# Last scan group's norms in fewer pieces, a ninth early block in the up projection, and a fourth buffer for weight differences

## The chip, the cores and the metric

The kernel runs on one core of a Trainium2 chip. The metric is device time in microseconds of one execution of the whole program, taken as the median of several runs. The profile of one execution shows five engines: PE (TensorE, matmuls) with its weight loads PEld, DVE (VectorE), ACT (ScalarE), POOL (GpSimd) and SP (SyncE), which issues DMAs.

## The reference

One layer of a two-branch encoder over 1024 rows of width 1024, float32. Cut to what the change touches:

```python
# branch B, the scan: forward and backward, 8 groups of 256 columns, 8 chunks of 128 rows
y = y_fwd + y_bwd + d_skip[:, None] * xs
y = y.reshape(b, l, D_INNER) * jax.nn.silu(z)
yg = y.reshape(b, l, SSD_GROUPS, D_INNER // SSD_GROUPS)
yg = yg * lax.rsqrt(jnp.mean(yg * yg, axis=-1, keepdims=True) + EPS)
...
merged = sigmoid(gate_a) * (attn @ w_attn_branch) + sigmoid(gate_b) * (ssd @ w_ssd_branch)
x = x + merged @ w_out
x = x + cross_attention(...)
h = rmsnorm(x, norm_ffn)
x = x + jnp.square(jax.nn.relu(h @ w_up)) @ w_down      # w_up 1024 x 4096
```

## The kernel before

The phases follow each other: the scan branch together with the gates' projection, attention, merge, cross attention, the up projection, the down projection. Every float32 matmul is three fast ones on a high and a low part (`mm3`, lines 83, 87 and 88); ACT writes the rounded high part and DVE or POOL the remainder. PE's order is as the code writes it; on the other engines a scheduler sets the order, and `issue_after(x)` keeps what is issued under it behind instruction x on the engine of x alone.

**The scan.** `step(q, c)` does chunk c of group q: a mask product (`cb`), products into the same tile, and `yo`, which needs a PSUM bank of a pool "p" of four that the gates' projection (`gps`, line 83 and on) shares. DVE and POOL finish the chunk (`yz`), ACT squares and sums it (`zs`, line 631). When four chunks are done, `rstd_of` gives their norm (DVE `rv`, line 120; POOL power `rr`, line 122) and ACT scales each `yz`. `yt(q)` transposes the four into two banks (line 650), and ACT copies these out (`yts`, line 652). The steps of the last group run between the products of the last gate jobs: `job(gate_job(10), {3: [...]})` puts its calls behind the job's third group of three matmuls. In the last group chunks 7 to 4 are normed together, and each of chunks 3 to 0 alone (`norm_one`, line 643), one step late.

**The up projection.** It is one level of the Strassen-Winograd scheme: 16 blocks of w_up's columns, each a "quad" of seven products of 12 matmuls (line 1412), in the order P1, P2, P6, P5, P7, P3, P4. P1 and P2 need only the input as it is; the others need sums of its quarters (`s1` to `s4`), which `sums` makes as the input rows become ready. So `ahead` does P1 and P2 of some blocks early, between the calls of `sums`: x = P1 is stored (`u`), P1 + P2 is added (line 1441) and squared (lines 1417 and 1418, ACT). Such a block's quad comes last, has five products, and fetches x back. The weights come in 512 KB loads on SP's queue (`raw`, two buffers and two shared ones); `right` makes a quad's differences t5 to t8 on DVE (lines 1385, 1386, 1388, 1391), and `put` splits each on ACT and POOL into `wop` (six buffers, lines 1357 and 1358). `start(order, 5)` issues the first five operands of the quads, `more` one more behind each product. The stores of results, the fetches and the weight loads are all issued by SP, one behind the other.

In the quads, line 1474 copies P1, line 1477 adds P2, line 1489 adds P7 (`c22`), line 1464 adds x in the quads of early blocks, and line 1493 adds P3. During the last three quads the first rows of the down projection are loaded (`sraw`) and split.

Of the kernel before, what the change touches and what calls it, by code (L numbers as in the profile page):

```python
# [16 lines left out]
P = 128  # L17
# [432 lines left out]
def ssd_phase(kx, ins, dr):  # L450
# [4 lines left out]
    with tc.tile_pool(name="p1", bufs=1) as sp, tc.manual_schedule(engines={mybir.EngineType.PE}):  # L455
# [138 lines left out]
        def step(q, c):  # L594

            b, j = c // 4, c % 4
            cl = slice(c * P, (c + 1) * P)
            cb, ef = q.cb, q.efs[c]
            if c:
                mask(q, c - 1)  # L600
            if c > 1:
                prep(q, c - 2)
            if j == 3:
                q.yz, q.ss = [None] * 4, sp.tile([P, 4], F32, tag="ss", bufs=2, name="ss")
            for h in range(4):
                PE.matmul(cb[:, 256 + 64 * h:256 + 64 * h + 64], ef[:, h], q.xtok[:, c, 64 * h:64 * h + 64],  # L606
                          start=True, stop=True)
            lo, hi = (256 if c == 0 else 0), (256 if c == NT - 1 else 512)
            yo = kx.pp.tile([P, 512], F32, tag="p", name="yo")
            PE.matmul(yo[:, lo:hi], q.CT[:, cl], q.prev[:, c].rearrange("p d q -> p (d q)")[:, lo:hi],  # L610
                      start=True, stop=True)
            d0, d1 = lo // 256, hi // 256
            t = sp.tile([P, 2, 256], F32, tag="t", bufs=1, name="t")
            V.tensor_tensor(t[:, d0:d1].rearrange("p d (h q) -> p d h q", h=4),
                            yo[:, lo:hi].rearrange("p (d h q) -> p d h q", h=4, q=64),
                            kx.ecs[:, b, j, d0:d1, q.hs].unsqueeze(3).broadcast_to([P, d1 - d0, 4, 64]), ALU.mult)
            single = q.g == NG - 1 and b == 0
            if single and j < 3:
                norm_one(q, j + 1)
            p1 = sp.tile([P, 256], F32, tag="p1", bufs=2, name="p1")  # L620
            G.tensor_tensor(heads(p1), heads(q.xtok[:, c]), dsk[:, q.hs].unsqueeze(2).broadcast_to([P, 4, 64]), ALU.mult)
            if d1 - d0 == 2:
                G.tensor_tensor(p1, p1, t[:, 1], ALU.add)
            if c > 1:
                with tc.issue_after(q.shut.ins):
                    back(q, c - 1)
            y = q.yz[j] = sp.tile([P, 256], F32, tag="yz", bufs=8, name="yz")
            V.tensor_tensor(y, cb[:, 256:], t[:, d0], ALU.add)
            V.tensor_tensor(y, y, p1, ALU.add)
            V.tensor_tensor(y, y, q.zs[:, c], ALU.mult)  # L630
            A.activation(q.zs[:, c], y, AF.Square, accum_out=q.ss[:, j:j + 1])
            if single and j == 0:
                norm_one(q, 0)
                q.done = b, q.yz
            elif not single and j == 0:
                r = rstd_of(kx, sp, q.ss, 4, 256, 4 * EPS)
                for i in range(4):
                    A.activation(q.yz[i], q.yz[i], AF.Copy, scale=r[:, i:i + 1])
                q.done = b, q.yz

        def norm_one(q, j):
            r = rstd_of(kx, sp, q.ss[:, j:j + 1], 1, 256, 4 * EPS)
            A.activation(q.yz[j], q.yz[j], AF.Copy, scale=r[:, 0:1])

        def yt(q):
            b, yz = q.done
# [29 lines left out]
            job(z_job(q), at)  # L676
        q = gs[7]
        job(gate_job(8), {5: [(step, q, 7)], 10: [(step, q, 6)], 15: [(step, q, 5)]})
        job(gate_job(9), {4: [(step, q, 4)], 9: [(step, q, 3)], 14: [(step, q, 2)]})
        job(gate_job(10), {3: [(yt, q), (step, q, 1)], 8: [(step, q, 0)]})  # L680
        w = jobs[0][0][0]()
        for n, ((_, run), at) in enumerate(jobs):
            nxt = jobs[n + 1][0][0]() if n + 1 < len(jobs) else None
# [503 lines left out]
def up_phase(kx, ins, dr, ok, grow, x1_low):  # L1187

    nc, tc = kx.nc, kx.tc
    with tc.tile_pool(name="p4", bufs=1, reuse_waits="tile") as mp:  # L1190
# [17 lines left out]
        with tc.tile_pool(name="tp", bufs=1, side="right", reuse_waits="tile") as tp:  # L1208
# [12 lines left out]
            up.sums(2, xns[0])  # L1221
            behind = up.turned
            up.ahead((5,))
            last = up.sums(3, xns[1])
            up.ahead((6, 7), behind)
            order = [b for b in range(16) if b not in up.early] + sorted(up.early)
            with tc.issue_after(last.ins):
                up.start(order, 5)
            stage = []
            for n, b in enumerate(order):  # L1230
                up.scalar = n > 11
                up.skip = 2 * (n == 14)
                if n == 13:
                    us, wd = down_tiles(kx)
                    wd = wd_views(wd[0])
                    raws = []

                    def load(src):
                        raws.append(mp.tile([P, D], F32, tag="ld", bufs=2, name="sraw"))
                        nc.sync.dma_start(raws[-1], src)  # L1240

                    def u_part(j):
                        split_u(kx, None, us, j, raws.pop(0))

                    def w_part(j):
                        split_wd(kx, None, wd[2 * j:2 * j + 2], j, raws.pop(0), nc.vector)

                    loads = [lambda j=j: load(dr.u[j]) for j in range(4)]
                    loads += [lambda j=j: load(ins["wdn"][j]) for j in range(2)]
                    splits = [lambda j=j: u_part(j) for j in range(4)] + [lambda j=j: w_part(j) for j in range(2)]  # L1250
                    stage += [loads[0], loads[1]]
                    for k in range(6):
                        stage.append(splits[k])
                        if k < 4:
                            stage[-1] = lambda k=k: (splits[k](), loads[k + 2]())
                up.quad(b, stage, order[n + 1] if n < 15 else None)
# [42 lines left out]
class Up:  # L1299
# [5 lines left out]
    def __init__(self, kx, ins, dr, mp, tp, s3, grow):  # L1305
        self.kx, self.ins, self.dr, self.mp, self.tp, self.s3, self.grow = kx, ins, dr, mp, tp, s3, grow
        s3["s2"] = kx.mp.tile([P, 4, 2, 512], F32R, tag="kt", bufs=4, name="kt")
        for key in ("s1", "s3", "s4", "a22"):
            s3[key] = mp.tile([P, 4, 2, 512], F32R, tag=key, bufs=1, name=key)
        self.early, self.scalar, self.skip = set(), True, 0  # L1310

    def t2(self, name):
        return self.tp.tile([P, 512], F32, tag="c", bufs=7, name=name)
# [55 lines left out]
    def right(self, order):  # L1369
# [7 lines left out]
        for n, b in enumerate(order):  # L1377
# [3 lines left out]
            if b not in self.early:  # L1381
                yield self.put(b11)
                yield self.put(b21)
            t5, t6, t7 = (self.tp.tile([P, 512], F32, tag="w", bufs=3, name="w") for _ in range(3))
            V.tensor_tensor(t5, b12, b11, ALU.subtract)
            V.tensor_tensor(t6, b22, t5, ALU.subtract)
            yield self.put(t6)
            V.tensor_tensor(t7, b22, b12, ALU.subtract)
            yield self.put(t5)
            yield self.put(t7)  # L1390
            V.tensor_tensor(t6, b21, t6, ALU.subtract)
            yield self.put(b22)
            yield self.put(t6)
            if n == 14:
                nxt = load(15)

# [3 lines left out]
            self.more()  # L1400

    def more(self):
        w = next(self.gen, None)
        if w is not None:
            self.ready.append(w)

# [21 lines left out]
    def ahead(self, bs, behind=None):  # L1428
# [3 lines left out]
        for b in bs:  # L1432
# [5 lines left out]
            kx.nc.scalar.activation(x, pb, AF.Copy)  # L1438
            kx.nc.sync.dma_start(self.dr.u[2 * b + 1][:, :512], x)
            self.product(pd, w[2], 2, True)  # L1440
            kx.nc.vector.tensor_tensor(c11, x, pd, ALU.add)
            self.square(c11, b, 0, 0)
            self.early.add(b)

    def quad(self, b, stage, nxt):
        kx = self.kx
# [438 lines left out]
```

## Time and profile before

| | |
|---|---|
| median of 3 runs | 2322.02 us (2321.02 to 2322.73) |
| the profiled execution: time, span | 2320.58 us, 2318.8 us |
| mean granted clock of PE | 0.996 |
| busy: PE, DVE, ACT, POOL | 2292.3, 1588.0, 1171.9, 932.0 us |
| PE's longest waits | 7.6 us (up projection), 5.2 us (last scan group) |

A line of the timeline reads: start, duration, engine, line of the kernel, operation, output <- inputs, shape, how many were drawn together, and in brackets the idle time of that engine just before and what ended it. A line of the waits gives the waiting tile, the work that ended the waits, the total, how many there were, and the longest. PEclk is the clock that PE was granted, as a share of its full speed.

### The profile page before, as it was taken

The page shows a single profiled execution, that of the slowest core. Times are in us where ns is not written, and L with a number is a line of the kernel's source. Part 1 is how long each engine was busy: PE and PEld are TensorE (multiplying, and loading weights), DVE is VectorE, ACT ScalarE, POOL GpSimd, SP SyncE. Part 2 cuts the span into 40 slices and gives each one's busy share as a digit, 9 for nine tenths or more (in the row PEclk, how much of TensorE's full clock was granted, in tenths as well). Part 3 has the DMA queues.
Part 4 walks back from the last instruction along what each step waited for, and adds up shares of the span by engine and source line. Part 5 has one row for each costly group of instructions (what it writes and reads, how often), then busy time and mean ns, then how long its engine had stood idle before and what let it go on. Part 6 is the DMA issues. An engine that isn't in the chain of part 4 may idle for free.

```text
span 2318.8 us, 32456 instructions
## 1 busy us (share of the span) xinstructions
PE 2292.3 (99%) x11882; PEld 1944.8 (84%) x11882; DVE 1588.0 (68%) x2501; ACT 1171.9 (51%) x2486; POOL 932.0 (40%) x887
## 2 busy tenths in 40 slices
PE   9999999999999999999999999999989999999998
PEld 8888898988889897888888888888968887888887
DVE  5877666677766673467659888865664456589984
ACT  5455655655465555488865442445553334233341
POOL 2355746565564754354540021125664444100010
PEclk9999999999999999999999999999999999999999
DMA  6222324232232323111144257011453345712201
GB/s 234 82 83 92 110 73 118 74 107 85 91 110 73 112 79 100 40 44 37 51 159 173 91 202 250 30 44 63 144 164 109 109 141 184 288 73 98 112 28 73
DMA packets 150322, 251.04 MB, mean 108 GB/s; under 512 B 11409, under 2 KB 86289, under 8 KB 150162
## 3 DMA queue, kind: packets, MB, share of 16 engines
q1 hardware_dynamic: 79408, 210.41, 26.8%
q10 hardware_dynamic: 70754, 38.55, 5.8%
q8 instruction: 94, 1.54, 0.3%
q14 instruction: 66, 0.54, 0.1%
HBM read 201.47 MB, written 47.45 MB: 107 GB/s over the span
## 4 chain that ended last, share of the span: by engine, by line
PE 87%; DVE 4%; ACT 3%; issue 2%; POOL 2%; DMA 2%; ACTq 0%; POOLq 0%; SPq 0%; DVEq 0%
PE mps L1625 10%; PE dps L1625 10%; PE pb L1412 6%; PE cps L83 4%; PE cps L88 4%; PE cps L87 4%; PE pc L1412 3%; PE zp L83 2%; PE zp L88 2%; PE zp L87 2%; PE cb L606 2%; PE yo L610 2%; PE gps L83 2%; PE gps L88 2%; PE gps L87 2%
## 5 line engine op out<-in xcount | busy, mean ns | idle before, releaser
L67 POOL TENSOR_TENSOR wlo<-raw,whi 128x1024 fp32r<-128x1024 f32 x96 | 235.7, 2456 | 385.6 <-ACT whi L64 310.8
L1576 ACT ACTIVATE kt<-row 128x512 fp32r<-128x512 f32 x264 | 143.8, 619 | 183.5 <-PE dps L1625 82.9
L1625 PE MATMUL mps<-kt 128*128 128x512 f32 x1008 | 229.7, 389 | 0.0
L1625 PE MATMUL dps<-kt 128*128 128x512 f32 x1008 | 228.6, 389 | 0.0
L1625 PEld LDWEIGHTS dps<-kt 128*128 128x128 f32 x1008 | 189.2, 188 | 39.3
L1625 PEld LDWEIGHTS mps<-kt 128*128 128x128 f32 x1008 | 189.0, 188 | 39.1
L83 PE MATMUL cps<-kt,whi 128*128 128x512 f32 x512 | 215.2, 420 | 0.0
L88 PE MATMUL cps<-kt,wlo 128*128 128x512 f32 x512 | 200.0, 391 | 0.0
L87 PE MATMUL cps<-kt,whi 128*128 128x512 f32 x512 | 199.2, 389 | 0.0
L64 ACT ACTIVATE whi<-raw 128x1024 fp32r<-128x1024 f32 x104 | 109.6, 1054 | 147.2 <-DMA raw<-in_wa_dram 26.8
L1577 DVE TENSOR_TENSOR kt<-row,kt 128x512 fp32r<-128x512 f32 x264 | 171.4, 697 | 3.8 <-ACT kt L1576 3.7
L548 POOL TENSOR_TENSOR xl<-xs,xh 128x512 fp32r<-128x512 f32 (+1 forms) x64 | 85.9, 1343 | 105.3 <-ACT xh L547 76.9
L122 POOL TENSOR_TENSOR rr<-rv,mhalf 128x1 f32<-128x1 f32 (+1 forms) x52 | 35.6, 686 | 227.5 <-DVE rv L120 220.4
L1358 POOL TENSOR_TENSOR wop<-w,wop 128x512 fp32r<-128x512 f32 x64 | 83.9, 1314 | 91.3 <-ACT wop L1357 83.9
L87 PEld LDWEIGHTS cps<-kt,whi 128*128 128x128 f32 x512 | 96.3, 188 | 25.3 <-issue 6.7
L83 PEld LDWEIGHTS cps<-kt,whi 128*128 128x128 f32 x512 | 96.3, 188 | 25.0 <-issue 6.0
L88 PEld LDWEIGHTS cps<-kt,wlo 128*128 128x128 f32 x512 | 96.1, 188 | 20.7
L583 ACT ACTIVATE ef<-rows,ebias 128x128 f32<-128x128 f32 x256 | 91.1, 393 | 34.7 <-PE cb L606 28.7
L809 DVE CUSTOM_DVE_ANT_0 t<-sps,bias,snk 128x384 f32<-128x384 f32 (+1 forms) x128 | 71.4, 581 | 52.4 <-PE sps L808 51.7
L817 POOL TENSOR_SCALAR t<-t,den 128x384 f32<-128x384 f32 (+1 forms) x128 | 69.2, 560 | 90.2 <-DVE den L815 81.2
L1412 PE MATMUL pb<-kt,wop 128*128 128x512 f32 x384 | 95.8, 399 | 8.1 <-ACT c L1474 7.6
L83 PE MATMUL gps<-kt,whi 128*128 128x512 f32 x240 | 103.7, 432 | 0.0
(393 smaller groups left out, 6491.0 us busy)
## 6 DMA issues: line engine op xcount, KB each, us to landing
rows<-d_cs ACTq DMA_DIRECT2D x128, 256.0 KB, 3.9
raw<-in_wssd_dram SPq DMA_DIRECT2D x48, 512.0 KB, 3.8
raw<-in_wup_dram SPq DMA_DIRECT2D x40, 512.0 KB, 4.1
d_u<-c SPq DMA_DIRECT2D x64, 256.0 KB, 2.3
row<-in_wdn_dram SPq DMA_DIRECT2D x28, 512.0 KB, 6.5
row<-d_u SPq DMA_DIRECT2D x28, 512.0 KB, 6.8
x<-in_x_dram SPq DMA_DIRECT2D x16, 512.0 KB, 6.5
raw<-in_wg_dram SPq DMA_DIRECT2D x16, 512.0 KB, 3.7
```

Source lines behind the costliest of these rows:

```text
L64: steps = [nc.scalar.activation(hi, raw, AF.Copy)]
L67: steps.append((eng or nc.gpsimd).tensor_tensor(lo, raw, hi.bitcast(F32), ALU.subtract))
L83: i = mm(out, l[0], r[0], start=first, stop=False)
L87: mm(out, l[0], r[1], start=False, stop=False)
L88: mm(out, l[1], r[0], start=False, stop=last)
L548: G.tensor_tensor(xl[:, lo:hi], xf[:, lo:hi], xh[:, lo:hi].bitcast(F32), ALU.subtract)
L583: A.activation(ef[:, h], rows[:, 0, h], AF.Exp, bias=kx.ebias[:, b, j, 0, o:o + 1])
L1358: self.kx.nc.gpsimd.tensor_tensor(t[:, 1], src, t[:, 0].bitcast(F32), ALU.subtract)
L1412: self.kx.nc.tensor.matmul(ps, w[:, i, ks], act[:, k, j], start=start and k == 0 and m == 0, stop=k == 3 and m == 2, skip_group_check=True)
L1576: nc.scalar.activation(t[:, j, 0], src, AF.Copy)
L1577: nc.vector.tensor_tensor(t[:, j, 1], src, t[:, j, 0].bitcast(F32), ALU.subtract)
L1625: self.kx.nc.tensor.matmul(ps[t], lt[:, k, x, ts], rt[:, k, y], start=n in (1, 2, 5) and k == 0 and m == 0, stop=k == 3 and m == 2, skip_g ...
```

## The change

It has three parts. In the last scan group chunks 3 to 1 are normed in one piece, in step 0, with chunk 0 still alone; `scale_rows` takes the place of `norm_one`, and the transposes of chunks 7 to 4 are called in the job before, two groups ahead of step 2, instead of just ahead of step 1. In the up projection block 8 becomes a ninth early block, behind the last `sums`; the first quad is then block 9's. The first operands of the quads are held behind the add of block 7, and those that `more` issues in the first quad behind the add of block 8. In `right`, t8 has a buffer of its own, the fourth of its tag, instead of being written over t6. Lines after the change are 1 lower than before at the end of the scan (yt is line 649, yts 651), and 3 to 5 higher in the up projection.

```diff
--- before.py
+++ after.py
@@ -615,8 +615,8 @@
                             yo[:, lo:hi].rearrange("p (d h q) -> p d h q", h=4, q=64),
                             kx.ecs[:, b, j, d0:d1, q.hs].unsqueeze(3).broadcast_to([P, d1 - d0, 4, 64]), ALU.mult)
             single = q.g == NG - 1 and b == 0
-            if single and j < 3:
-                norm_one(q, j + 1)
+            if single and j == 0:
+                scale_rows(q, 1, 3)
             p1 = sp.tile([P, 256], F32, tag="p1", bufs=2, name="p1")
             G.tensor_tensor(heads(p1), heads(q.xtok[:, c]), dsk[:, q.hs].unsqueeze(2).broadcast_to([P, 4, 64]), ALU.mult)
             if d1 - d0 == 2:
@@ -630,17 +630,16 @@
             V.tensor_tensor(y, y, q.zs[:, c], ALU.mult)
             A.activation(q.zs[:, c], y, AF.Square, accum_out=q.ss[:, j:j + 1])
             if single and j == 0:
-                norm_one(q, 0)
+                scale_rows(q, 0, 1)
                 q.done = b, q.yz
             elif not single and j == 0:
-                r = rstd_of(kx, sp, q.ss, 4, 256, 4 * EPS)
-                for i in range(4):
-                    A.activation(q.yz[i], q.yz[i], AF.Copy, scale=r[:, i:i + 1])
+                scale_rows(q, 0, 4)
                 q.done = b, q.yz
 
-        def norm_one(q, j):
-            r = rstd_of(kx, sp, q.ss[:, j:j + 1], 1, 256, 4 * EPS)
-            A.activation(q.yz[j], q.yz[j], AF.Copy, scale=r[:, 0:1])
+        def scale_rows(q, j, n):
+            r = rstd_of(kx, sp, q.ss[:, j:j + n], n, 256, 4 * EPS)
+            for i in range(n):
+                A.activation(q.yz[j + i], q.yz[j + i], AF.Copy, scale=r[:, i:i + 1])
 
         def yt(q):
             b, yz = q.done
@@ -676,8 +675,8 @@
             job(z_job(q), at)
         q = gs[7]
         job(gate_job(8), {5: [(step, q, 7)], 10: [(step, q, 6)], 15: [(step, q, 5)]})
-        job(gate_job(9), {4: [(step, q, 4)], 9: [(step, q, 3)], 14: [(step, q, 2)]})
-        job(gate_job(10), {3: [(yt, q), (step, q, 1)], 8: [(step, q, 0)]})
+        job(gate_job(9), {4: [(step, q, 4)], 9: [(step, q, 3)], 12: [(yt, q)], 14: [(step, q, 2)]})
+        job(gate_job(10), {3: [(step, q, 1)], 8: [(step, q, 0)]})
         w = jobs[0][0][0]()
         for n, ((_, run), at) in enumerate(jobs):
             nxt = jobs[n + 1][0][0]() if n + 1 < len(jobs) else None
@@ -1221,13 +1220,17 @@
             up.sums(2, xns[0])
             behind = up.turned
             up.ahead((5,))
-            last = up.sums(3, xns[1])
-            up.ahead((6, 7), behind)
+            up.sums(3, xns[1])
+            last = up.ahead((6, 7), behind)
+            up.hold = up.ahead((8,))
             order = [b for b in range(16) if b not in up.early] + sorted(up.early)
-            with tc.issue_after(last.ins):
-                up.start(order, 5)
+            hold, up.hold = up.hold, last
+            up.start(order, 5)
+            up.hold = hold
             stage = []
             for n, b in enumerate(order):
+                if n == 1:
+                    up.hold = None
                 up.scalar = n > 11
                 up.skip = 2 * (n == 14)
                 if n == 13:
@@ -1307,7 +1310,7 @@
         s3["s2"] = kx.mp.tile([P, 4, 2, 512], F32R, tag="kt", bufs=4, name="kt")
         for key in ("s1", "s3", "s4", "a22"):
             s3[key] = mp.tile([P, 4, 2, 512], F32R, tag=key, bufs=1, name=key)
-        self.early, self.scalar, self.skip = set(), True, 0
+        self.early, self.scalar, self.skip, self.hold = set(), True, 0, None
 
     def t2(self, name):
         return self.tp.tile([P, 512], F32, tag="c", bufs=7, name=name)
@@ -1381,16 +1384,16 @@
             if b not in self.early:
                 yield self.put(b11)
                 yield self.put(b21)
-            t5, t6, t7 = (self.tp.tile([P, 512], F32, tag="w", bufs=3, name="w") for _ in range(3))
+            t5, t6, t7, t8 = (self.tp.tile([P, 512], F32, tag="w", bufs=4, name="w") for _ in range(4))
             V.tensor_tensor(t5, b12, b11, ALU.subtract)
             V.tensor_tensor(t6, b22, t5, ALU.subtract)
             yield self.put(t6)
             V.tensor_tensor(t7, b22, b12, ALU.subtract)
             yield self.put(t5)
             yield self.put(t7)
-            V.tensor_tensor(t6, b21, t6, ALU.subtract)
+            V.tensor_tensor(t8, b21, t6, ALU.subtract)
             yield self.put(b22)
-            yield self.put(t6)
+            yield self.put(t8)
             if n == 14:
                 nxt = load(15)
 
@@ -1400,7 +1403,8 @@
             self.more()
 
     def more(self):
-        w = next(self.gen, None)
+        with self.kx.tc.issue_after(self.hold.ins) if self.hold else ExitStack():
+            w = next(self.gen, None)
         if w is not None:
             self.ready.append(w)
 
@@ -1438,9 +1442,10 @@
             kx.nc.scalar.activation(x, pb, AF.Copy)
             kx.nc.sync.dma_start(self.dr.u[2 * b + 1][:, :512], x)
             self.product(pd, w[2], 2, True)
-            kx.nc.vector.tensor_tensor(c11, x, pd, ALU.add)
+            added = kx.nc.vector.tensor_tensor(c11, x, pd, ALU.add)
             self.square(c11, b, 0, 0)
             self.early.add(b)
+        return added
 
     def quad(self, b, stage, nxt):
         kx = self.kx
```

On PE, at the last scan group, before: the end of the groups ahead of step 1, the transposes (line 650), and the step.

```order
L87 MATMUL gps<-kt,whi 128x512
L88 MATMUL gps<-kt,wlo 128x512
L83 MATMUL gps<-kt,whi 128x512
L87 MATMUL gps<-kt,whi 128x512
L88 MATMUL gps<-kt,wlo 128x512
L650 MATMUL yt<-ident,yz 128x128 x8
L590 MATMUL cb<-cC,cB 128x128
L606 MATMUL cb<-xtok,ef 128x64 x4
L610 MATMUL yo<-prev,cC 128x512
```

After: the same instructions (now line 649) two groups ahead of step 2, whose `cb` is the seventh row behind them.

```order
L83 MATMUL gps<-kt,whi 128x512
L87 MATMUL gps<-kt,whi 128x512
L88 MATMUL gps<-kt,wlo 128x512
L649 MATMUL yt<-ident,yz 128x128 x8
L83 MATMUL gps<-kt,whi 128x512
L87 MATMUL gps<-kt,whi 128x512
L88 MATMUL gps<-kt,wlo 128x512
L83 MATMUL gps<-kt,whi 128x512
L87 MATMUL gps<-kt,whi 128x512
L88 MATMUL gps<-kt,wlo 128x512
L590 MATMUL cb<-cC,cB 128x128
L606 MATMUL cb<-xtok,ef 128x64 x4
```

The transposes passed six matmuls and step 2 and the five groups behind it; nothing else moved on PE there.

On ACT at the passage to the quads, before (x is the copy of an early block's P1, the last row the first quad's copy of its own P1):

```order
L1438 ACTIVATE x<-pb 128x512
L1334 ACTIVATE s_16493<-f_17021 128x4x128
L1417 ACTIVATE c_17050<-c_17050 128x512
L1418 ACTIVATE c_17050<-c_17050 128x512
L1357 ACTIVATE wop<-w 128x512
L1438 ACTIVATE x<-pb 128x512
L1357 ACTIVATE wop<-w 128x512 x2
L1357 ACTIVATE wop<-raw 128x512
L1417 ACTIVATE c_17092<-c_17092 128x512
L1418 ACTIVATE c_17092<-c_17092 128x512
L1474 ACTIVATE c_17154<-pb 128x512
```

After, from block 7's copy x on (c_17084 is block 7's and c_17126 block 8's sum):

```order
L1442 ACTIVATE x<-pb 128x512
L1421 ACTIVATE c_17084<-c_17084 128x512
L1422 ACTIVATE c_17084<-c_17084 128x512
L1360 ACTIVATE wop<-w 128x512 x2
L1442 ACTIVATE x<-pb 128x512
L1360 ACTIVATE wop<-w 128x512
L1360 ACTIVATE wop<-raw 128x512
L1421 ACTIVATE c_17126<-c_17126 128x512
L1422 ACTIVATE c_17126<-c_17126 128x512
L1479 ACTIVATE c_17189<-pb 128x512
```

Block 7's relu and square follow its copy directly, and block 8's stand between the last weight copies and the first quad's copy.

On DVE at the same place, before; c_17050 is block 6's sum and c_17092 block 7's, and `w` are the weight differences:

```order
L1441 TENSOR_TENSOR c_17050<-x,pd 128x512
L1385 TENSOR_TENSOR w<-raw 128x512
L1335 TENSOR_TENSOR s_16493<-f_17021,s_16493 128x4x128
L1386 TENSOR_TENSOR w<-raw,w 128x512
L1388 TENSOR_TENSOR w<-raw 128x512
L1391 TENSOR_TENSOR w<-raw,w 128x512
L1385 TENSOR_TENSOR w<-raw 128x512
L1441 TENSOR_TENSOR c_17092<-x,pd 128x512
L1386 TENSOR_TENSOR w<-raw,w 128x512
L1388 TENSOR_TENSOR w<-raw 128x512
L1477 TENSOR_TENSOR c_17154<-c_17154,pd 128x512
```

After; c_17042, c_17084 and c_17126 are the sums of blocks 6, 7 and 8:

```order
L1445 TENSOR_TENSOR c_17042<-x,pd 128x512
L1338 TENSOR_TENSOR s_16485<-f_17013,s_16485 128x4x128
L1445 TENSOR_TENSOR c_17084<-x,pd 128x512
L1388 TENSOR_TENSOR w<-raw 128x512
L1389 TENSOR_TENSOR w<-raw,w 128x512
L1391 TENSOR_TENSOR w<-raw 128x512
L1445 TENSOR_TENSOR c_17126<-x,pd 128x512
L1394 TENSOR_TENSOR w<-raw,w 128x512
L1388 TENSOR_TENSOR w<-raw 128x512
L1389 TENSOR_TENSOR w<-raw,w 128x512
```

Block 7's add stood behind five differences and stands now ahead of all; three of them are ahead of block 8's add.

In the first full quad on DVE, before (line 1489 adds P7):

```order
L1477 TENSOR_TENSOR c_17154<-c_17154,pd 128x512
L1420 SCALAR_TENSOR_TENSOR c_17154<-c_17154 128x512
L1391 TENSOR_TENSOR w<-raw,w 128x512
L1489 TENSOR_TENSOR c_17224<-c_17224,pb 128x512
L1420 SCALAR_TENSOR_TENSOR c_17224<-c_17224 128x512
L1385 TENSOR_TENSOR w<-raw 128x512
```

After (line 1388 is t5 of the next block's weights, line 1494 adds P7):

```order
L1482 TENSOR_TENSOR c_17189<-c_17189,pd 128x512
L1424 SCALAR_TENSOR_TENSOR c_17189<-c_17189 128x512
L1388 TENSOR_TENSOR w<-raw 128x512
L1494 TENSOR_TENSOR c_17259<-c_17259,pb 128x512
L1424 SCALAR_TENSOR_TENSOR c_17259<-c_17259 128x512
L1389 TENSOR_TENSOR w<-raw,w 128x512
```

The first difference of the next weights passed ahead of the addition of P7; before, it came behind it.

## The prediction

> **What bounds the kernel now.** I read the page's busy times and its chain first, then the waits of PE (TensorE), then the granted clock around the longest of those waits, then the timelines there.
>
> ```profile
> span 2318.8 us, 32456 instructions
> PE 2292.3 (99%) x11882; PEld 1944.8 (84%) x11882; DVE 1588.0 (68%) x2501; ACT 1171.9 (51%) x2486; POOL 932.0 (40%) x887
> PE 87%; DVE 4%; ACT 3%; issue 2%; POOL 2%; DMA 2%; ACTq 0%; POOLq 0%; SPq 0%; DVEq 0%
> ```
>
> PE is busy for 2292.3 of 2318.8 us, so a change that leaves its matmuls as they are can win two things only: the 26.5 us in which PE stands, and the time in which it runs at a lowered clock. This change leaves the matmuls as they are: the early products of a block replace the same products of its later quad. So I look for the waits of PE that it touches.
>
> ```profile
> engine line waited for: us in total, times, longest us
> PE pb L1412 <- ACT c L1474: 7.6, 1, 7.6
> PE yo L610 <- ACT yts L652: 5.2, 1, 5.2
> PE pb L1412 <- DVE c L1489: 1.4, 1, 1.4
> PE pb L1412 <- DVE c L1464: 1.1, 2, 0.8
> ```
>
> The two longest happen once each, the first at the passage from early blocks to quads in the up projection, the second at the end of the last scan group. Those are the two places the change rewrites. Call them B and A. What they cost beside the standing time is in the windows around them (stretch, its length, five engines' busy time, PEclk, DMA share, GB/s).
>
> ```profile
> core 0: us, PE busy (x) PEld busy (x) DVE busy (x) ACT busy (x) POOL busy (x), PEclk, DMA share, GB/s
> 885.00:890.00 5.00, 5.00 (x30) 4.09 (x28) 2.80 (x6) 2.48 (x7) 3.10 (x3) 1.00 0.00 0
> 890.00:895.98 5.98, 0.80 (x9) 0.69 (x7) 1.60 (x4) 3.90 (x9) 4.18 (x4) 0.95 0.53 153
> 895.98:899.00 3.02, 3.02 (x6) 1.75 (x7) 0.90 (x2) 0.43 (x1) 0.17 (x1) 0.53 0.96 330
> 1722.00:1729.45 7.45, 0.00 (x1) 0.01 (x1) 5.10 (x5) 3.93 (x9) 5.83 (x4) 0.69 0.38 113
> 1729.45:1734.73 5.28, 5.28 (x12) 4.14 (x13) 3.04 (x3) 0.98 (x2) 2.52 (x2) 0.50 0.39 140
> 1734.73:1737.71 2.98, 2.98 (x14) 2.41 (x12) 0.00 (x0) 1.12 (x2) 1.29 (x1) 0.94 0.24 88
> 1950.04:1953.00 2.96, 2.96 (x13) 2.42 (x14) 1.14 (x2) 2.82 (x6) 0.43 (x1) 1.00 0.85 308
> ```
>
> After each long wait PE comes back at about half speed. At A the clock is 0.53 for 3.02 us, a loss of 3.02 x 0.47 = 1.4 us; at B it is 0.50 for 5.28 us and 0.94 for 2.98 us, a loss of 2.64 + 0.18 = 2.8 us. Behind the 1.4 us wait on line 1489, which ends at 1950.04, the clock stays at 1.00. So A costs 5.2 + 1.4 = 6.6 us and B 7.6 + 2.8 = 10.4 us, and a wait of about 1.4 us costs only itself.
>
> **A, the last scan group.** The change norms chunks 1 to 3 in one piece, and moves the transposes of chunks 4 to 7 (yt) from just ahead of step 1 to two matmul groups ahead of step 2.
>
> ```profile
> 881.93 0.39 PE L83 MATMUL gps<-kt,whi 128*128 128x512 f32 x1
> 888.70 1.04 PE L650 MATMUL yt<-ident,yz 128*128 128x128 f32 x8
> 889.57 0.39 PE L590 MATMUL cb<-cC,cB 128*128 128x128 f32 x2
> 895.98 2.05 PE L610 MATMUL yo<-prev,cC 128*128 128x512 f32 x2 [5.18 <-ACT yts L652]
> 882.70 1.71 ACT L638 ACTIVATE yz<-yz,rr 128x256 f32<-128x256 f32 x4 [2.19 <-POOL rr L122]
> 894.75 0.51 ACT L643 ACTIVATE yz<-yz,rr 128x256 f32<-128x256 f32 x1 [2.08 <-POOL rr L122]
> 895.16 1.25 ACT L652 ACTIVATE yts<-yt,cols 128x512 f32<-128x512 f32 x2
> 891.86 2.34 POOL L67 TENSOR_TENSOR wlo<-raw,whi 128x1024 fp32r<-128x1024 f32 x1
> 894.16 0.55 POOL L122 TENSOR_TENSOR rr<-rv,mhalf 128x1 f32<-128x1 f32 x1
> ```
>
> The chain of the stall reads backwards: yo (895.98) needs the PSUM bank that the copy yts (895.16) empties; the copy stands on ACT behind a single norm (894.75), which waits for its POOL power (894.16), which stands behind a 2.34 us weight split (891.86). With the edit the power and norm of chunk 2 are no longer ahead of the copies on ACT, and the transposes lie some 30 matmuls earlier. What is new is that PE may reach them too soon. It is at 881.93 at their new place, and the four normed chunks are written from 882.70 to 884.41. The last two transposes start some 0.2 us after that (the copy's first half ends near 895.79, and PE takes its bank at 895.98) and take 2/8 of the 0.87 us that the eight took (888.70 to 889.57): done at 884.82. The stretch is 2.9 us, of which 0.87 is PE's own work: a new wait of 2.0 us in pieces, the longest about 1.3 (881.93 to the first chunk near 883.2). The matmuls queued behind the waiting transposes lose the same 2.0 and no more. For the bank that step 2's yo then takes I allow 0.3; its bounds are 0 and 1.2 (the two copies' 1.25 us in the way). At the end of the group the last transposes still wait for chunk 0's norm, as before; chunks 1 to 3 are due before it. A: -6.6 + 2.0 + 0.3 = **-4.3**, between -6.6 and -2.0.
>
> The Trainium skill, "TensorE: Matmul & The Clock Gate" (Part 1), says that the clock halves after an idle window of about 3.4 us; the trace agrees, with 5.2 and 7.6 us trips and none at 1.4. By its Part 4, PE-mode transposes do not count as busy; then the stretch at the new place would be one of about 3 us without counted work. No row here shows that; by it A is a rival below.
>
> **B, first quad of the up projection.** The ninth early block (8) puts two products of block 9 between block 8's early ones and the first quad's P6; the weight differences of that quad are held, on DVE, until block 7's add, and later ones until block 8's.
>
> ```profile
> 1716.27 2.88 PE L1412 MATMUL pb<-kt,wop 128*128 128x512 f32 x12
> 1718.99 2.88 PE L1412 MATMUL pd<-kt,wop 128*128 128x512 f32 x12
> 1729.45 5.49 PE L1412 MATMUL pb<-kt,wop 128*128 128x512 f32 x12 [7.57 <-ACT c L1474]
> 1720.74 0.68 DVE L1386 TENSOR_TENSOR w<-raw,w 128x512 f32<-128x512 f32 x1
> 1723.52 1.74 DVE L1391 TENSOR_TENSOR w<-raw,w 128x512 f32<-128x512 f32 x1 [1.50 <-POOL wop L1358]
> 1725.18 1.74 DVE L1385 TENSOR_TENSOR w<-raw 128x512 f32<-128x512 f32 x1
> 1726.85 0.68 DVE L1441 TENSOR_TENSOR c<-x,pd 128x512 f32<-128x512 f32 x1
> 1721.99 0.58 ACT L1438 ACTIVATE x<-pb 128x512 f32<-128x512 f32 x1
> 1727.62 0.63 ACT L1417 ACTIVATE c<-c 128x512 f32<-128x512 f32 x1 [3.49 <-DVE c L1441]
> 1728.82 0.58 ACT L1474 ACTIVATE c<-pb 128x512 f32<-128x512 f32 x1
> ```
>
> Read backwards again: PE waits for the copy c (1728.82), which follows on ACT the relu and square (1727.62) of block 7, which wait for the DVE add at 1726.85, which stands behind the differences at 1723.52 and 1725.18, the first of which waits for POOL to have read t6. After the change PE has the two products of block 9 as well, so it comes to P6 one pair later, at 1716.27 + 4 x 2.72 = 1727.15 (2.72 is the distance of the first two rows). On DVE block 7's add runs once x is there, near 1721.7 (its copy now starts about 1 us earlier than 1721.99, since ACT has one weight copy fewer ahead of it); three differences at 0.68 end at 1723.8, block 8's add at 1724.5; if one or two run at the 1.74 of the slow rows, 1725.8. Relu and square (2 x 0.63) and the copy (0.58) follow: 1726.3 to 1727.7. Wait 0 to 0.6; I take 0.6, since two of the three differences read here were slow ones. B: -10.4 + 0.6 = **-9.8**.
>
> What the ninth block adds: one more x stored and fetched back (256 KB each way) and one 512 KB weight load moved ahead; DVE adds in place of ACT copies. The load was issued about four products ahead, and PE's own 10.9 us cover its landing; without that cover it would show at P1 of block 9. The fetch is wanted only at the very end.
>
> **The fourth buffer and the rest of the quads (C).** t8 no longer waits for POOL to read t6; those DVE waits were off PE's path, so by themselves they bring 0. But DVE's order in every quad moves: t5 of the next weights now stands ahead of the add that frees P4's operand.
>
> ```profile
> 1762.58 0.68 DVE L1385 TENSOR_TENSOR w<-raw 128x512 f32<-128x512 f32 x1
> 1748.79 0.33 SPq L1366 DMA_DIRECT2D raw<-in_wup_dram  x1
> raw<-in_wup_dram SPq DMA_DIRECT2D x40, 512.0 KB, 4.1
> 2035.31 5.45 DVE L1650 TENSOR_TENSOR x<-x,dps 128x512 f32<-128x512 f32 x8 [0.55 <-PE dps L88]
> ```
>
> Those weights are issued at 1748.79, land 4.1 us later near 1753, and are read at 1762.58: 9.7 us of slack cover the move by a few us. The waits on lines 1489 and 1464 at the end (1.4 + 1.1 = 2.5 us) lie where DVE's order changes too; they may vanish or double, -2.5 to +2.5, and nothing says which: 0. Block 8 is now the last quad, so its rows for the down projection come later; DVE has other work there until the adds at 2035.31, so I charge 0.
>
> Sum: -4.3 - 9.8 + 0 = -14.1. The profiled execution took 2320.58 us, 1.4 under the median 2322.02: it becomes 2306.5, and the median 2307.9.
>
> **The rivals.**
> (1) The transposes do not hold the clock, so the stretch of about 3 us at A's new place lowers it. For it: A's own idle tripped it inside 5.2 us. Against: its idle pieces are 1.3 us and less, and 1.4 did not trip. Price as after A's wait now, 1.4, or as B's, 2.8: 2309.3 to 2310.7.
> (2) B's chain stays long: all three differences run at 1.74, 3.2 us more, so the wait is near 3.8, and the clock falls, 2.8 more. For it: two such rows stand there now. Against: the hold puts block 7's add ahead of them. -14.1 + 6.0: 2313.9.
> (3) A's wait only changes place: step 2's yo waits for a bank behind the copies, or PE for the yz a little later, 1 to 2.3 us more: 2309 to 2310.2.
> (4) Slower: t5, ahead of line 1489's add on DVE, waits for its raw weights in every full quad, and P4 with it. Seven quads have to lose 14.1 us to undo the gain, 2.0 each, and 2.7 each for slower by 0.2%. For it: the queue that issues those loads also waits for stores. Against: 9.7 us of slack. At 3 us in each of seven: 2329.
>
> **The numbers.** Forecast 0.66, rivals 0.12, 0.10, 0.08, 0.04. Of the forecast alone the range is 2302.5 (A and B wholly gone and C's 2.5 too: -19.5) to 2311. Holding eight in ten and the first three rivals, it is 2302.5 to 2315. What a measurement can tell from no change is about 0.2%, 4.6 us: faster means under 2317.4. The forecast, (1) and (3) lie below it; of (2) I put half above, since a longer wait adds its own size: faster 0.91, same 0.05, slower 0.04.
>
> **What would show it.** In the profile after: no wait of 7.6 us on the copy and none of 5.2 on yts; a wait of yt on yz of up to 2 us near 882 to 885; PEclk 1.00 right behind both places; the products of the full quads still 2.7 us apart. It is wrong if a long wait of P6 on ACT remains, if PEclk drops near 885, or if every quad shows a wait on line 1489's successor.

## Result: 2308.5 us against 2322.1, and the profile after

The changed kernel takes 2308.50 us (median of 6 runs, 2306.48 to 2310.98), the one before 2322.08 (6 runs). The ratio is 0.9943, with a 95% interval of 0.993 to 0.9956: 13.6 us, or 0.6%, faster. The profiled execution took 2306.48 us with a span of 2304.7, 14.1 less than before. The head of its page, and the longest waits of PE:

```profile
span 2304.7 us, 32485 instructions
PE 2288.2 (99%) x11882; PEld 1941.3 (84%) x11882; DVE 1582.1 (69%) x2501; ACT 1173.3 (51%) x2486; POOL 935.3 (41%) x885
...
PE pb L1416 <- DVE c L1469: 1.6, 1, 1.6
PE pc L1416 <- DVE c L1469: 1.1, 2, 0.9
...
PE pb L1416 <- ACT c L1479: 1.1, 1, 1.1
...
PE yt L649 <- ACT yz L642: 0.7, 1, 0.7
```

The waits of 7.6 and 5.2 us are gone; 1.1 and 0.7 stand in their places. PE is also busy for 4.1 us less (2288.2 against 2292.3) with the same 11882 matmuls, since it no longer runs at half speed behind those waits.

At A, the last scan group, PE and ACT after the change, and the clock:

```profile
881.38 0.39 PE L88 MATMUL gps<-kt,wlo 128*128 128x512 f32 x1
882.47 1.96 PE L649 MATMUL yt<-ident,yz 128*128 128x128 f32 x8 [0.70 <-ACT yz L642]
885.66 0.39 PE L590 MATMUL cb<-cC,cB 128*128 128x128 f32 x2
886.75 1.10 PE L610 MATMUL yo<-prev,cC 128*128 128x512 f32 x2
881.91 1.70 ACT L642 ACTIVATE yz<-yz,rr 128x256 f32<-128x256 f32 x4 [1.56 <-POOL rr L122]
885.93 0.67 ACT L651 ACTIVATE yts<-yt,cols 128x512 f32<-128x512 f32 x1
881.60:885.66 4.06, 3.15 (x15) 2.15 (x15) 1.14 (x3) 3.75 (x10) 1.59 (x3) 1.00 0.01 2
```

PE waits 0.70 for the first normed chunk, then its eight transposes take 1.96 us in place of 1.04, since ACT delivers the chunks 0.4 us apart. The first copy ends near 886.60 and yo takes a bank at 886.75 without a wait. From step 3's cb to step 0's yo it is 24.7 us before (877.89 to 902.58) and 19.8 after (877.57 to 897.34): A brought 4.9 us.

At B, the passage to the quads, PE, DVE, ACT and the clock behind it:

```profile
1719.25 2.88 PE L1416 MATMUL pd<-kt,wop 128*128 128x512 f32 x12
1723.19 3.04 PE L1416 MATMUL pb<-kt,wop 128*128 128x512 f32 x12 [1.06 <-ACT c L1479]
1726.06 2.96 PE L1416 MATMUL pc<-s,wop 128*128 128x512 f32 x12
1715.88 0.69 DVE L1445 TENSOR_TENSOR c<-x,pd 128x512 f32<-128x512 f32 x1 [0.80 <-ACT x L1442]
1720.46 0.69 DVE L1445 TENSOR_TENSOR c<-x,pd 128x512 f32<-128x512 f32 x1 [1.10 <-ACT x L1442]
1718.79 1.15 ACT L1360 ACTIVATE wop<-w 128x512 fp32r<-128x512 f32 x2 [0.89 <-DVE w L1389]
1719.85 0.58 ACT L1442 ACTIVATE x<-pb 128x512 f32<-128x512 f32 x1
1722.56 0.58 ACT L1479 ACTIVATE c<-pb 128x512 f32<-128x512 f32 x1
1723.19:1726.06 2.87, 2.87 (x12) 2.36 (x13) 2.77 (x3) 0.98 (x2) 2.87 (x3) 1.00 0.00 0
```

Block 7's add runs at 1715.88, right behind its copy; block 8's waits for its copy x (1719.85), which stands on ACT behind two weight copies that wait for a difference. Relu, square and the first quad's copy follow, and P6 has waited 1.06 us, at full clock. From block 7's second product to the first quad's P5 it was 21.2 us for four products (1713.55 to 1734.73), and is 17.7 for six (1708.37 to 1726.06). With 2.72 us a product that is 10.3 us too much before and 1.4 after; P5 itself was 0.2 longer before. B brought 9.1 us.

At the end of the up projection PE's waits are 2.7 us in all, as many as before and in other places, and the down projection's adds start with the same 0.55 us gap as before:

```profile
1932.48 3.02 PE L1416 MATMUL pc<-s,wop 128*128 128x512 f32 x12 [0.90 <-DVE c L1469]
1946.87 3.03 PE L1416 MATMUL pc<-s,wop 128*128 128x512 f32 x12 [0.20 <-DVE c L1469]
1959.84 3.02 PE L1416 MATMUL pb<-s,wop 128*128 128x512 f32 x12 [1.64 <-DVE c L1469]
2021.19 5.45 DVE L1655 TENSOR_TENSOR x<-x,dps 128x512 f32<-128x512 f32 x8 [0.55 <-PE dps L88]
```

### The profile page after: what moved, and what is told of

Same layout as the page of the kernel before. It is cut to its first block, busy times and chain, and to the rows that moved or that the text cites. A ratio compares the mean times of both kernels' runs of the same rounds, so it can differ in the third digit from the quotient of the medians.

```text
span 2304.7 us, 32485 instructions
## 1 busy us (share of the span) xinstructions
PE 2288.2 (99%) x11882; PEld 1941.3 (84%) x11882; DVE 1582.1 (69%) x2501; ACT 1173.3 (51%) x2486; POOL 935.3 (41%) x885
## 4 chain that ended last, share of the span: by engine, by line
PE 88%; DVE 4%; ACT 2%; DMA 2%; issue 1%; POOL 1%; ACTq 0%; SPq 0%; POOLq 0%; DVEq 0%
PE mps L1630 10%; PE dps L1630 10%; PE pb L1416 6%; PE cps L83 4%; PE cps L88 4%; PE cps L87 4%; PE pc L1416 3%; PE zp L83 2%; PE zp L88 2%; PE zp L87 2%; PE cb L606 2%; PE yo L610 2%; PE gps L83 2%; PE gps L88 2%; PE gps L87 2%; PE mps L87 1%
## 5 line engine op out<-in xcount | busy, mean ns | idle before, releaser
L122 POOL TENSOR_TENSOR rr<-rv,mhalf 128x1 f32<-128x1 f32 (+2 forms) x50 | 34.6, 694 | 226.1 <-DVE rv L120 224.3
L584 ACT ACTIVATE eb<-rows,ebias 128x128 f32<-128x128 f32 x256 | 89.9, 394 | 30.2 <-POOL rows L576 30.1
L1299 POOL TENSOR_TENSOR wd<-row,wd 128x1024 fp32r<-128x1024 f32 x4 | 11.1, 2794 | 228.4 <-ACT wd L1298 228.4
```

Of the source, the lines that this page charges most:

```text
L584: A.activation(eb[:, h], rows[:, 1, h], AF.Exp, bias=kx.ebias[:, b, j, 1, o:o + 1])
```

## The experiments

The theory: each of the two waits had a cause of its own in the order on one engine (ACT at A, DVE and then ACT at B), and each also cost its stretch at the lower clock. Rivals are told with each run. Ratios are to the kernel before, run on the same chip.

**The parts by themselves.** First the scan's hunks of the change alone, then those of the up projection alone:

```diff
 # scan only: the change without
-            up.hold = up.ahead((8,))
-        with self.kx.tc.issue_after(self.hold.ins) if self.hold else ExitStack():
-            t5, t6, t7, t8 = (... bufs=4 ...)
 # up projection only: the change without
-                scale_rows(q, 1, 3)
-        job(gate_job(9), {..., 12: [(yt, q)], ...})
```

> Only the scan part of the change; the up projection as before. Theory (each of the two long waits had its own cause, and their prices add): 4.9 us faster than before, the yts wait of 5.2 gone, the copy wait of 7.6 still there. Rival (the scan's gain is given back later, at a wait that the phases behind it share): under 2 us faster.

> Only the up projection's parts (ninth block, hold, fourth buffer); the scan as before. Theory: 9.2 us faster than before, the yts wait of 5.2 still there, P6's wait about 1.1. Rival (gain partly lent by the scan's): 5 us faster or less.

Scan only: ratio 0.9985 (0.9976 to 0.9994), median 2.8 us below before; P6's wait is 7.6, yts' gone, and the stretch from step 3's cb to step 0's yo is 20.0 us against 24.7. Up only: 0.9963 (0.995 to 0.9975), 8.4 us below; waits 4.9 (yts) and 1.1 (P6). Both intervals hold the expected 4.9 and 9.2 us (ratios 0.9979 and 0.9960), and the two ratios multiply to 0.9948, beside the changed kernel's 0.9943. Within these intervals the prices add. The stretches say so more sharply: A's is 20.0 us in the first, and B's, from block 7's second product to P5, 17.7 in the second, against 19.8 and 17.7 in the changed kernel.

**Either half of A.** The grouped norms with the transposes at their old place, and the new place with single norms:

```diff
 # norms only: scale_rows as in the change, but
+        job(gate_job(10), {3: [(yt, q), (step, q, 1)], 8: [(step, q, 0)]})
 # place only: norm_one as before, but
+        job(gate_job(9), {4: [(step, q, 4)], 9: [(step, q, 3)], 12: [(yt, q)], 14: [(step, q, 2)]})
```

> Only the norms of chunks 3 to 1 in one piece; the transposes stay ahead of step 1. Theory (the copies waited because a single norm stood ahead of them on ACT): the copies then stand behind a weight split and two gate copies only and start near 891.5, so yo waits 1 to 2 us and the clock stays: 4 to 5.5 us faster. Rival (the place of the transposes is what counts): the wait stays over 3.5 us and the clock falls, under 2 us faster.

> Only the transposes moved two groups ahead of step 2; each of chunks 3 to 0 is normed alone as before. Theory: the copies now precede every single norm on ACT, so the wait is gone too, 1.8 us of new cost at the new place: 4.5 to 5 us faster. Rival (the single norms, still waiting for POOL with gate copies and weight splits behind them on ACT, stop PE elsewhere): a wait of 2 us or more on gt, whi or yz later, under 3 us faster.

PE at yo of step 1 and a little later with the norms only, and at the transposes with the place only:

```profile
892.49 1.10 PE L610 MATMUL yo<-prev,cC 128*128 128x512 f32 x2 [1.88 <-ACT yts L651]
893.96 0.63 PE L88 MATMUL gps<-kt,wlo 128*128 128x512 f32 x1
```

```profile
882.79 1.96 PE L650 MATMUL yt<-ident,yz 128*128 128x128 f32 x8 [0.79 <-ACT yz L638]
```

Norms only: the wait is 1.9, as expected, but the clock does not stay. It is 0.50 from 893.77 to 897.19, and a matmul then takes 0.63 us in place of 0.39. The stretch is 21.6 us, 3.1 less than before, under the expected 4 (ratio 0.9987, 0.9978 to 0.9996): 1.6 us are lost behind the wait, where before it was 1.4. Place only: 19.9 us, as good as both together, and no new wait (0.998, 0.9971 to 0.9989). So either half ends the long wait, since each takes the single norm out from in front of the copies. The norms alone leave 1.9 us of it and the slow stretch; the place does all of it, and with it the grouped norms add nothing that shows.

**The ninth block and the holds.**

```diff
 # no ninth block
-            up.hold = up.ahead((8,))
 # no holds
-        with self.kx.tc.issue_after(self.hold.ins) if self.hold else ExitStack():
+        with ExitStack():
```

> The changed kernel without the ninth early block: the first quad is block 8's, its first differences held on DVE behind block 7's add, four buffers, the scan as changed. Theory A (the wait came from DVE's order, block 7's add behind the differences): P6 waits only for add, relu, square and copy after block 7's last product, 1.5 to 2.5 us, at full clock; at most 1.5 us slower than the changed kernel. Theory B (the products of one more block are the cover): the wait grows by a pair of products against the changed kernel's 1.1, to 5 us and more, and the clock falls; 6 to 10 us slower than the changed kernel.

> The changed kernel without the holds: ninth early block, four buffers and the scan as changed, but DVE's differences placed freely; five of them then stand ahead of block 7's add, the fifth waiting for a buffer that POOL reads. Theory A (DVE's order): block 7's add comes near 6 us later, block 8's too, P6 waits 4 to 8 us and the clock falls; 6 to 10 us slower than the changed kernel. Theory B (the pair's cover): P6 waits under 2.5 us; at most 1.5 us slower.

Without the ninth block (ratio 0.9966, 0.9952 to 0.9979), PE, ACT, DVE and the clock behind P6:

```profile
1721.08 5.49 PE L1415 MATMUL pb<-kt,wop 128*128 128x512 f32 x12 [3.44 <-ACT c L1478]
1716.83 0.69 DVE L1444 TENSOR_TENSOR c<-x,pd 128x512 f32<-128x512 f32 x1 [0.80 <-ACT x L1441]
1718.88 1.67 ACT L1359 ACTIVATE wop<-w 128x512 fp32r<-128x512 f32 x3
1720.46 0.57 ACT L1478 ACTIVATE c<-pb 128x512 f32<-128x512 f32 x1
1721.08:1726.37 5.29, 5.29 (x13) 4.13 (x13) 5.06 (x4) 1.51 (x3) 5.29 (x5) 0.50 0.30 98
```

Block 8's add is gone with its early products, and with it the hold on the later differences. Block 7's add is early, and yet P6 waits 3.4 us: three weight copies stand on ACT between block 7's square and the first quad's copy. That is enough for the clock to fall. Counted as above, 6.4 us are lost, 5.0 more than with the ninth block, and the median is 5.6 above the changed kernel's 2308.5. Without the holds (0.9987, 0.9979 to 0.9996):

```profile
1732.91 4.94 PE L1416 MATMUL pb<-kt,wop 128*128 128x512 f32 x12 [9.10 <-ACT c L1479]
1722.54 1.77 DVE L1388 TENSOR_TENSOR w<-raw 128x512 f32<-128x512 f32 x1 [1.19 <-POOL wop L1361]
1724.23 0.68 DVE L1445 TENSOR_TENSOR c<-x,pd 128x512 f32<-128x512 f32 x1
1728.72 1.73 DVE L1391 TENSOR_TENSOR w<-raw 128x512 f32<-128x512 f32 x1 [3.21 <-POOL wop L1361]
1730.38 0.68 DVE L1445 TENSOR_TENSOR c<-x,pd 128x512 f32<-128x512 f32 x1
```

Both early adds (1724.23, 1730.38) stand again behind differences that wait for POOL, and P6 waits 9.1 us, longer than in any other run and than the 4 to 8 expected: the pair of products is eaten whole. 10.2 us above the changed kernel. Neither theory holds alone. Of the 10.5 us at B the ninth block without the holds saves nothing, the holds without the ninth block 4.1, and both 9.1: the hold frees the chain, and the pair covers what ACT still has in it.

**Three buffers, and a tenth block.**

```diff
 # three buffers
-            V.tensor_tensor(t8, b21, t6, ALU.subtract)
+            V.tensor_tensor(t6, b21, t6, ALU.subtract)
 # a tenth block
-            up.hold = up.ahead((8,))
+            up.hold = up.ahead((8, 9))
```

> The changed kernel with three buffers for the differences, t8 written over t6 as before. Theory (DVE's waits for POOL are off PE's path): DVE waits for POOL on t8 in most quads again, P6's wait stays near 1.1, the time is within 1.5 us of the changed kernel. Rival (the fourth buffer carries part of the gain): 3 us slower or more.

> The changed kernel with a tenth early block (9) behind block 8, the first quad's held differences behind block 9's add. Theory (what is left of P6's wait is the chain add, relu, square, copy of the last early block, which moves along with it): P6 still waits 0.7 to 1.5 us, within 1 us of the changed kernel. Rival (each further pair is further cover): the 1.1 us is gone, 1 us faster.

With three buffers the median is 2312.73, 4.2 us above the changed kernel's, as the rival had it (ratio 0.9956, 0.9943 to 0.9968). But the five runs lie apart, at 2307.7 and 2308.0 and at 2312.7 to 2314.3, and the profile shows one of the lower. There P6 waits 1.1 as with four, and the span of 2306.2 us is 1.5 over the changed kernel's: 1.3 were lost ahead of the last scan group (878.85 at step 3's cb against 877.57) and 0.4 in it. That the buffer costs nothing on PE's path is shown for that execution; the upper three, and with them the rival, stay open.

With ten early blocks P6 waits 1.8 in place of 1.1, more than the theory's 0.7 to 1.5, and the median is 3.2 us above the changed kernel's, where within 1 was expected (0.9954, 0.9941 to 0.9966). The chain moves with the last early block, as the theory said, and further pairs bring nothing. This execution lost more at A, and at a wait of 2.3 us on line 1469 (1.6 in the changed kernel), behind which the clock was 0.50 from 1964.31 to 1967.73. At A, PE and the clock with ten blocks, and behind them PE in the run without holds, whose code at A is the same:

```profile
883.85 1.97 PE L649 MATMUL yt<-ident,yz 128*128 128x128 f32 x8 [1.29 <-ACT yz L642]
885.57 0.66 PE L83 MATMUL gps<-kt,whi 128*128 128x512 f32 x1
885.20:888.16 2.96, 2.96 (x11) 2.40 (x11) 1.03 (x2) 2.96 (x8) 0.68 (x1) 0.58 0.00 0
```

```profile
884.49 1.96 PE L649 MATMUL yt<-ident,yz 128*128 128x128 f32 x8 [1.29 <-ACT yz L642]
886.21 0.48 PE L83 MATMUL gps<-kt,whi 128*128 128x512 f32 x1
```

The same wait and the same transposes: once the clock falls to 0.58, once not. This is the prediction's first rival, in one execution and not in the other.

**Do transposes hold the clock?** The last eight transposes of the scan seven times over, where no wait precedes them:

```diff
-                for j in range(4):
+                for j in [0, 1, 2, 3] * (7 if q.g == NG - 1 and b == 0 else 1):
```

> The changed kernel with the last eight transposes of the scan done seven times over, into the same banks: 56 in a row, 48 more, about 5.2 us at the 0.109 us of one, with no wait in front or between. It asks whether transposes alone hold PE's clock. Theory (they do not; that is how the clock once fell behind a wait of 1.3 us and 1.7 us of transposes): the granted clock falls within or behind the stretch, the first matmuls after it take over 0.6 us in place of 0.39, 2 to 3 us lost, so 7 to 8 us slower than the changed kernel. Rival (they hold it): 1.00 throughout, 5.2 us slower.

```profile
906.62 6.28 PE L649 MATMUL yt<-ident,yz 128*128 128x128 f32 x56
912.96 0.39 PE L87 MATMUL qps<-kt,whi 128*128 128x512 f32 x1
906.62:912.65 6.03, 6.03 (x58) 6.03 (x56) 0.00 (x0) 2.68 (x4) 2.37 (x1) 1.00 0.51 145
912.65:915.50 2.85, 2.85 (x16) 2.34 (x15) 0.00 (x0) 0.69 (x1) 0.00 (x0) 1.00 0.65 246
```

They hold it: 6.03 us of nothing but transposes at 1.00, and the matmuls behind them at 0.39. The theory of this run falls, in this execution. It was 6.1 us slower than the changed kernel (0.9967, 0.9955 to 0.9979); 5.2 are the added transposes, and at A this execution lost 2.3 more, with a wait of 1.45.

**What is left at A and B.** The transposes behind step 2; the same with block 8 squared on DVE; and the changed kernel once more:

```diff
-        job(gate_job(9), {..., 12: [(yt, q)], 14: [(step, q, 2)]})
+        job(gate_job(9), {..., 14: [(step, q, 2)], 15: [(yt, q)]})
 # and, in the second,
+            up.scalar = False
             up.hold = up.ahead((8,))
```

> The changed kernel with the transposes of chunks 7 to 4 one group behind step 2 instead of two groups ahead of it. Theory (the 1.8 us left at this place is PE arriving ahead of the normed chunks): they are ready, no wait, and the copies still end before step 1's yo asks for a bank near 890; from step 3's cb to step 0's yo it is 18.0 us in place of 19.8; about 1.8 us faster than the changed kernel, a little more where the clock fell there. Rival (the bank wait returns, since the copies now stand behind a weight split and a square on ACT): a wait of yo on yts over 1 us, no gain.

> As the run with the transposes behind step 2, and the ninth block's square on DVE in one instruction instead of relu and square on ACT. Theory (P6 waits for relu and square of block 8, which stand ahead of the first quad's copy on ACT): the copy comes 1.2 us earlier and P6's wait of 1.1 us is gone; 2.9 us faster than the changed kernel in all. Rival (DVE's 1.1 to 1.5 us more delay the differences): a new wait of P5 or P7 on wop, under 2 us faster.

> The changed kernel itself, on the same chip as the two above, for their comparison: 2307 to 2312 us; its profile shows again the waits of 1.1 (P6) and 0.7 to 1.3 us (transposes).

PE with the transposes behind step 2; at P2 and P6 in the run with both; and at the transposes in the changed kernel again, with its clock:

```profile
886.74 0.60 PE L649 MATMUL yt<-ident,yz 128*128 128x128 f32 x4
889.22 0.66 PE L649 MATMUL yt<-ident,yz 128*128 128x128 f32 x4 [1.88 <-DVE t L614]
```

```profile
1722.42 2.88 PE L1417 MATMUL pd<-kt,wop 128*128 128x512 f32 x12
1725.14 3.04 PE L1417 MATMUL pb<-kt,wop 128*128 128x512 f32 x12
```

```profile
884.87 2.52 PE L649 MATMUL yt<-ident,yz 128*128 128x128 f32 x8 [1.52 <-ACT yz L642]
887.04 0.78 PE L83 MATMUL gps<-kt,whi 128*128 128x512 f32 x1
883.40:887.00 3.60, 1.92 (x8) 1.35 (x9) 0.60 (x2) 2.70 (x8) 2.18 (x3) 0.87 0.01 2
887.00:889.62 2.62, 2.62 (x8) 2.09 (x7) 1.03 (x2) 2.62 (x7) 1.12 (x1) 0.53 0.00 0
```

The later place trades the wait for another: the second four transposes need the bank of step 2's yo, which DVE reads late, 1.9 us. The stretch is 20.1 us, no shorter than the 19.8, though the clock stayed. The square on DVE does what was expected, P6 follows P2 without a wait, but a 1.8 us wait on P7's add (line 1495) stands in this execution's list. In time: 2307.49 (ratio 0.9942, 0.9929 to 0.9956), 2307.72 (0.9947, 0.9935 to 0.996), and 2308.56 for the changed kernel (0.9944, 0.9932 to 0.9957). Neither version can be told from the changed kernel.

## Why the prediction was right, and where it was off

The forecast was 2307.9 us, the median 2308.5. The profiled execution became 2306.5 as worked out, but its terms were off against each other: A by -0.6, B by +0.7, C by +0.2, and 0.3 came ahead of A (step 3's cb at 877.57 against 877.89). The agreement to a tenth of a microsecond is luck; six runs of the changed kernel lie between 2306.48 and 2310.98.

**A, -4.3 forecast, -4.9 measured.** What the old wait cost was right: from step 3's cb to step 2's it is 8.1 us after, against a step's 5.4 and the transposes' 0.9, so 1.8 too much; without these 1.8 the stretch of 19.8 is 18.0, and the 24.7 of before exceeds it by 6.7 against 6.6. The new wait was put at 2.0 and came to 1.8; the 0.3 allowed for yo's bank was not needed, and rival (3) did not come. (The bound of -2.0 does not follow from the working, whose terms give -3.4 at worst.) The size differs by execution: with the changed order at A the stretch was 19.8, 20.0, 19.8, 20.4 and 20.2 us in five, with waits of 0.7 to 1.3, and 21.9, 22.1 and 22.1 in three, with waits of 1.3 to 1.5. In those three the clock fell; one of them is the changed kernel's second profile, so the sign "PEclk drops near 885" came in one of its two profiles. Rival (1) was right in kind there, and its price of 1.4 to 2.8 holds the 1.6 to 1.8 us by which they exceed the longest of the others.

Its reason, as it was put, was not. By the Trainium skill, "TensorE: Matmul & The Clock Gate" (Part 4), PE-mode transposes do not count as PE-busy the same way; here 56 in a row counted enough to keep the clock at 1.00, in one execution. Nor does PE's busy share of the stretch decide: from the start of the wait to the end of the transposes PE was busy for 1.51 of 3.01 us with ten blocks, where the clock fell, and for 1.50 of 3.00 without the holds, where it stayed.

What differs is where the stretch lies in time. In each of the fourteen traces every change of the granted clock comes at a whole number of steps of 3.41 us from every other, on a fixed raster: the low stretches between 30 and 2300 us last 3.41, 6.83 or 10.24 us, and the falls are whole steps apart (in the kernel before, 895.43 to 1724.87 is 243 of them). With ten blocks one step, from 882.29 to 885.70, held the whole wait and all eight transposes, with 1.91 us of PE work, and the next step ran at 0.50. Without the holds the same wait and transposes lay across two steps, with 2.89 and 2.43 us of PE work, and the clock stayed. In that part of the traces, steps at full clock with at most 1.2 us of PE work were all followed by a fall, and steps with 2.0 or more by none. Between 1.4 and 2.0 both happened, so what exactly is counted, and how much a transpose counts, stays open; no run moved the stretch against the raster and nothing else.

**B, -9.8 forecast, -9.1 measured.** The mis-sized terms are the 10.4 of before, which by the distance of the products is 10.5, and P6's wait, put at 0 to 0.6 and measured at 1.06; the remaining 0.3 us lies around that wait (P2 and P6 start 3.94 apart, 1.22 over the usual 2.72) and in P6 itself, 2.87. The step that failed is what block 8's add waits for. I had it behind three differences on DVE; it waited 1.10 us for its copy x on ACT, which stood behind two weight copies, which waited for t6 on DVE. The working also left out the 0.68 us of block 7's own add; with it the wait comes to 0 to 1.2, which holds the 1.06, but by a chain that was not the one that ran. The cover and the hold were right as a pair, and the run without the ninth block shows how near the edge it was: 3.4 us of wait, and the clock with it. Rival (2) needed such a wait and did not come.

**C, 0 forecast, +0.2 measured** from the waits on line 1469 (2.7 us against 2.5). The full quads show no wait of P4, so t5's new place was covered, and rival (4) fell. The fourth buffer did not end DVE's waits for POOL. In us in total, times, longest:

```profile
DVE w L1388 <- POOL wop L1361: 37.1, 13, 5.4
DVE w L1394 <- POOL wop L1361: 33.8, 10, 4.8
DVE w L1391 <- POOL wop L1361: 9.1, 6, 2.1
```

With line 1389's 8.7 that is 88.7 us on the four differences, where the kernel before had 102.1. With three buffers and the rest of the change it is 87.7, so the buffer moved waits from t7 (31.7 with three, 9.1 with four) to t5 (10.1 and 37.1) and did not shorten them in all. None of PE's longest waits in the changed kernel is for these differences.

The step that I did not have is the scatter: the code ahead of the last scan group is the same in all these kernels, yet step 3's cb came between 877.6 and 882.4 us. That and the clock at A make up a spread that is as large as A's whole price.

## What to carry to other kernels

When PE is busy for 99% of the time, price a wait by its own time and by the slow stretch behind it, and look for what stands ahead of the releasing instruction on its own engine: here a norm that waited for POOL, and an add behind differences that weren't due. Cover and order have to come together: the same pair of products was worth nothing while the add stood behind the differences, and 5 us once it did not. A move that puts PE a little early at a new place should be read in several executions, since what PE then waits can differ by 0.8 us and the clock falls in some of them. A wait of 1 to 2 us is not safe by its length alone.

## What the runs showed of the hardware

Waits of 3.4 us and more (3.4, 4.9, 5.2, 7.4, 7.6, 9.1) were each followed by a clock near 0.5. Shorter ones went either way: a wait of 1.9 was followed by 0.50 with the norms only and by 1.00 with the transposes behind step 2, and one of 1.3 ahead of eight spread transposes by 0.50 with ten blocks and by 1.00 without the holds. The granted clock changed on a raster of 3.41 us within each execution, so a fall lasts one, two or three steps, and its price goes with that. Behind yts' wait the clock was low for one step in the kernel before (895.43 to 898.84), and 1.4 us were lost (6.6 us from step 1's yo to step 0's, against 5.2 at full clock). In the run with the up projection's parts alone it was low for two (894.43 to 901.26), and 2.8 us were lost (8.0 us). A run of 56 transposes over 6.03 us kept the clock at 1.00.
